# MLP down passes whose PSUM banks start from the sums so far, with more units by seven products

## The chip, the core and the metric

The kernel runs on one core of a Trainium2 chip. The metric is the device time of one execution in microseconds, the median of several. The profile is of one execution; TensorE is PE in it (its weight loads PEld), VectorE is DVE, ScalarE ACT, GpSimd POOL, and the queue of SyncE SP.

## What is computed

One layer of a trunk: a gated linear attention mixer, then a squared-ReLU MLP, each with an RMSNorm ahead and a residual behind, then a final RMSNorm. 256 tokens, 2048 channels, all float32. The change touches the MLP and the end only:

```python
def _sq_relu_mlp(h, w_up, w_down):      # w_up (2048, 8192), w_down (8192, 2048)
    a = jax.nn.relu(h @ w_up)
    return (a * a) @ w_down
...
    h = h + _sq_relu_mlp(_rmsnorm(h, mlp_norm[i]), mlp_w_up[i], mlp_w_down[i])
return _rmsnorm(h, final_norm)
```

## The kernel before

**Float32 from three products.** Each weight tile is loaded from HBM into a `raw` tile (six of them in turn). ACT writes its rounded part `hi`, DVE the rest `lo = raw - hi` (function `parts`, L117 and L118, for the down weights; `weights`, L137 and L141, for the up weights). A product is three matmuls: activation hi by weight hi, hi by lo, lo by hi. `hi` and `lo` each have five slots in turn (`slots`), so a new pair can be written when TensorE has done with the pair five before it. The activations are the stationary operand in the down passes; every matmul there has 256 columns.

**Rounds.** The hidden width of 8192 is cut into eight rounds m of 1024. `up` makes a round's hidden activations in 16 steps of 24 matmuls (two halves q of eight steps, each half with two PSUM banks). At the end of a half, `forms` takes each bank: a ReLU with the norm's factor on DVE (L700, tile `su`), the square on ACT (L704), and, where sums are needed, three subtractions on DVE (L708), then hi and lo of the result (L715, L716, tile `act`). Four such forms belong to a round.

**Down.** `down` walks through passes (m, g): round m, group g of 512 output columns. There are four groups in rounds 0 to 6, walked forward in odd rounds and backward in even ones (`order_of`), so that the last group of a round is the first of the next and the two passes share their banks; round 7 does only groups 0 and 1 in this way. A pass has four units kp, each one tile of 256 x 512 of `w_down`. One up step stands between two units, for as long as there are up steps: there are 128, and 18 are done ahead of the first unit, so the last ten of the 120 units have none.

**Two ways of a unit.** A plain unit multiplies a 2 x 2 arrangement of blocks with eight products, 24 matmuls. A unit by sums uses seven products of sums of blocks (the scheme of Strassen and Winograd), 21 matmuls: three products with the weights as loaded (9 matmuls, from 768 of the tile's 1024 columns), then four products with sums of weight blocks (12 matmuls). The sums are three additions on DVE (L770) into one of two `work` tiles, which then goes through hi and lo again (L117 and L118, the rows with `hi<-work` and `lo<-work`) into a slot of the ring. Which units go by sums is said by

```python
def by_sums(m, g, kp):
    if m == ROUNDS - 1:
        return (g, kp) in ((1, 0), (1, 2))
    return kp < (2 if g == 1 or m == ROUNDS - 2 else 3)
```

that is 11 of 16 units in rounds 0 to 5, eight in round 6, two of the eight in round 7: 76 in all.

**Banks.** A pass, or a pair of passes that share, adds up in four PSUM banks: `b16`, `b32`, `b57`, `bx4`. The first matmul in each overwrites. When the pass is over, its sums must be added to what earlier rounds left: `b32` and `bx4` to the two token halves of the residual `h` (`take`, L722), `b16` and `b57` to the group's `sums` (L802; the first time a plain copy on ACT, L800). These are additions on DVE out of PSUM, 23 passes' ends with four each; they are kept in `late` and put out two at a time by `settle` behind the next units. When a group is through, `combine` (L819, L823) adds its `sums` into `h`. PSUM has eight banks: four for the pass, two for the up step, and two that pass between them through the list `free`.

**The end.** The last two groups of round 7 are done in natural order (`last_step`) in five banks; each is added to `h` by `take` (L883), squared on ACT with a row sum (`finish`, L846) and multiplied by the final norm's gain on DVE (L848). From the row sums come `sf` (L886), its power -1/2 on POOL (`rsqrt`, L321), the scaling and the stores.

Engines execute their instructions in the order in which the build lays them down; an instruction that waits holds up those behind it on its engine. The build orders them itself within what `issue_after` prescribes.

Of the kernel before, what the change touches and what calls it, by code (L numbers as in the profile page):

```python
# [32 lines left out]
P = 128  # L33
T = 256
# [34 lines left out]
def tile_gla_mlp(ctx, tc, x, xt, cols, w_vg, w_in, w_gate, w_out, w_up, w_down, final_norm, out):  # L69
# [38 lines left out]
    last_load, last_hi, last_lo, last_sum = [None], [None], [None], [None]  # L108
# [4 lines left out]
    def parts(raw, n, to, pieces=None):  # L113

        hi, lo = to
        for s in (slice(*p) for p in pieces or [(0, n)]):
            last_hi[0] = nc.scalar.copy(hi[:, s], raw[:, s])  # L117
            last_lo[0] = nc.vector.tensor_tensor(lo[:, s], raw[:, s], hi[:, s].bitcast(F32), op=ALU.subtract)  # L118
        return hi, lo
# [4 lines left out]
    def weights(src, n, pieces=None, room=None, gap=None):  # L124
# [5 lines left out]
        for s in (slice(*p) for p in loads):  # L130
            dst = raw[:, s]
            if len(src.shape) == 3:
# [4 lines left out]
                last_hi[0] = nc.scalar.copy(to[0], dst)  # L137
# [530 lines left out]
    free = deque([*acc_free, *aux_free])  # L668

    def up():  # L670
        ended = []
        for m in range(ROUNDS):
            for q in range(MR // GT):
# [22 lines left out]
    def forms(m, kp, bank, act):  # L696
        ways = {by_sums(m, g, kp) for g in range(GROUPS)}
        f = work[:, 2].rearrange("p (f s) -> p f s", f=8)
# [4 lines left out]
        )  # L703
        nc.scalar.activation(  # L704
# [16 lines left out]
    def take(bank, t, lo, n):  # L721
        nc.vector.tensor_tensor(h[:, t, lo : lo + n], bank, h[:, t, lo : lo + n], op=ALU.add)  # L722

    left, right = slice(0, T), slice(T, 2 * T)
    used, begun = set(), set()
    n_sums = [0]

    def down(passes):

        late = []  # L730

        def settle(n=2):

            with tc.issue_after(last_lo[0].ins):
                for f in late[:n]:
                    f()
            del late[:n]

        for n, (m, g) in enumerate(passes):
            if not n or passes[n - 1][1] != g:  # L740
                taken = [free.popleft() for _ in range(2)]
                b16, b32 = (psum_bank(i) for i in taken)
                b57 = None
            ends = n + 1 == len(passes) or passes[n + 1][1] != g
            for kp in range(KP):
# [3 lines left out]
                def product(bank, o, a, w, c):  # L749
# [10 lines left out]
                w = parts(raw, 2 * GT, slots(), [(T * by_parts, 2 * GT)])  # L760
                if by_parts:
                    block = lambda i: slice(i * T, (i + 1) * T)
                    product(b16, left, at(A11), w, block(1))
                    product(b32, right, at(A12), w, block(3))
                    product(b32, left, at(S4), w, block(2))
# [10 lines left out]
                else:  # L776
                    for i in range(2):
                        for bank, f in ((b32, (A11, A12)), (bx4, (A21, A22))):
                            product(bank, slice(0, GT), at(f[i]), w, slice(i * GT, (i + 1) * GT))
                yield  # L780
                settle()
                if by_parts:
                    if b57 is None:
                        taken += [free.popleft() for _ in range(2)]
                        b57, bx4 = (psum_bank(i) for i in taken[2:])
# [3 lines left out]
                    product(b57, left, at(S1), wu, block(0))  # L789
                    product(b57, right, at(S3), wu, block(1))  # L790
                    product(b16, right, at(S2), wu, block(2))
                    product(bx4, right, at(A22), wu, block(3))
            if ends:

                e = sums[g]

                def keep(dst, b, first=g not in begun):
                    b = b.rearrange("p (f s) -> p f s", f=2)
                    if first:
                        nc.scalar.copy(dst, b)  # L800
                    else:
                        nc.vector.tensor_tensor(dst, b, dst, op=ALU.add)  # L802

                begun.add(g)
                fs = (
                    lambda keep=keep, b=b16, e=e: keep(e[:, 1:3], b),
                    lambda b=b32, g=g: take(b, 0, g * GT, GT),
                    lambda keep=keep, b=b57, e=e: keep(e[:, 0::3], b),
                    lambda b=bx4, g=g: take(b, 1, g * GT, GT),
                )  # L810
                late.extend(lambda f=f, i=i: (f(), free.append(i)) for f, i in zip(fs, taken))
                if m == ROUNDS - 1 or m == ROUNDS - 2 and g > 1:
                    late.append(lambda g=g: side.extend(combine(g)))
        settle(len(late))
# [15 lines left out]

    passes = [(m, g) for m in range(ROUNDS) for g in order_of(m) if m < ROUNDS - 1 or g < 2]
# [11 lines left out]

    def finish(t, lo, n):
        sq = tmp.tile([P, 512], F32, tag="t512", name="sqf", bufs=3)
        nc.scalar.activation(sq[:, :n], h[:, t, lo : lo + n], AF.Square, accum_out=fs[:, t, n_fs[t] : n_fs[t] + 1])  # L846
        n_fs[t] += 1
        nc.vector.tensor_tensor(hf[:, t, lo : lo + n], h[:, t, lo : lo + n], fb[:, lo : lo + n], op=ALU.mult)  # L848
# [86 lines left out]
```

## Time and profile before

| | |
|---|---|
| median of 3 runs | 1065.09 us (1065.07 to 1065.47) |
| profiled execution | 1064.77 us, of which 1062.8 us span |
| TensorE busy in the span | 1053.7 us |
| VectorE busy | 842.3 us |
| ScalarE busy | 590.2 us |
| HBM read | 206.92 MB, 197 GB/s |

A row of the groups has the line, the engine, the operation, output and inputs by the program's names, the shapes and the count; then busy time in us, the mean of one instruction in ns, and the idle time of the engine just before such instructions with what ended most of it. A row of the waits has who waited for whom, the total in us, how often, and the longest. A row of busy time by stretch has the stretch, its length, then the busy time of PE, PEld, DVE, ACT and POOL with the number of instructions in brackets, the granted clock, the DMA share and GB/s. A row of the timeline has start, length, engine and instruction. The busy time counts overlapping instructions of an engine once; the mean of a group is an instruction's own length. A matmul is pipelined: its own row shows 276 ns, while the next one starts after 113 ns.

### The profile page before, as it was taken

How to read it: one execution, taken by the hardware profiler on the slowest of the kernel's cores; microseconds unless marked ns; L12 is line 12 of the kernel's file. 1: busy time of each engine (PE TensorE's matmuls, PEld its weight loads, DVE VectorE, ACT ScalarE, POOL GpSimd, SP SyncE). 2: the span in 40 equal slices, each digit the busy share in tenths (PEclk: the TensorE clock that was granted, in tenths of full speed). 3: DMA queues.
4: the chain of work that ended last, by engine and by line, in shares of the span. 5: the costliest groups of instructions: out<-in, count | busy, mean ns of one | idle time of the engine just before them, and what ended most of it. 6: DMA issues, size and time to landing. Idle time of an engine off the chain costs nothing.

```text
span 1062.8 us, 22112 instructions
## 1 busy us (share of the span) xinstructions
PE 1053.7 (99%) x9202; PEld 1053.0 (99%) x9202; DVE 842.3 (79%) x1144; ACT 590.2 (56%) x723; POOL 13.2 (1%) x39
## 2 busy tenths in 40 slices
PE   9999999999999999999999999999999999999996
PEld 9999999999999999999999999999999999999996
DVE  5778644656555566898999999999999989979987
ACT  6785444545445454665655655655655556545454
POOL 0000000000000000000000000000000000000000
PEclk9999999999999999999999999999999999999999
DMA  9957765556656666666666666676667665666662
GB/s 337 325 164 218 198 189 155 160 156 178 196 180 185 184 179 187 174 194 200 213 214 194 201 202 198 198 229 191 193 198 223 194 203 186 213 198 198 211 220 86
DMA packets 94788, 210.45 MB, mean 198 GB/s; under 512 B 6704, under 2 KB 7600, under 8 KB 94560
## 3 DMA queue, kind: packets, MB, share of 16 engines
q1 hardware_dynamic: 93728, 206.99, 62.7%
q10 hardware_dynamic: 960, 2.05, 0.5%
q8 instruction: 72, 1.18, 0.5%
q14 instruction: 28, 0.23, 0.1%
HBM read 206.92 MB, written 2.10 MB: 197 GB/s over the span
## 4 chain that ended last, share of the span: by engine, by line
PE 97%; DMA 2%; issue 0%; SPq 0%; DVE 0%; ACT 0%; POOL 0%; POOLq 0%; DVEq 0%; ACTq 0%
PE acc L152 53%; PE up L189 33%; PE acc L189 6%; PE aux L189 2%; DMA raw<-in_w_vg 1%; PE aux L152 1%; PE aux L558 1%; DMA zz<-in_xt 1%; PE aux L486 1%; SPq L144 0%; DVE lo L118 0%; ACT hi L117 0%; POOL rf L321 0%; PE acc L387 0%; SPq L278 0%
## 5 line engine op out<-in xcount | busy, mean ns | idle before, releaser
L118 DVE TENSOR_TENSOR lo<-raw,hi 128x768 fp32r<-128x768 f32 (+3 forms) x226 | 251.5, 1115 | 124.4 <-ACT hi L117 123.5
L117 ACT CAST hi<-raw 128x768 fp32r<-128x768 f32 (+3 forms) x226 | 217.6, 965 | 202.5 <-PE acc L152 134.3
L152 PE MATMUL acc<-hi,act 128*128 128x256 f32 x1864 | 323.2, 276 | 0.0
L189 PE MATMUL up<-hl,hi 128*128 128x256 f32 x1024 | 282.9, 276 | 0.0
L189 PE MATMUL up<-hh,hi 128*128 128x256 f32 x1024 | 282.8, 277 | 0.0
L189 PE MATMUL up<-hh,lo 128*128 128x256 f32 x1024 | 282.5, 276 | 0.0
L152 PEld LDWEIGHTS acc<-hi,act 128*128 128x128 f32 x1864 | 274.7, 188 | 0.0
L137 ACT CAST hi<-raw 128x1024 fp32r<-128x1024 f32 x160 | 167.9, 1051 | 166.7 <-PE up L189 91.4
L141 DVE TENSOR_TENSOR lo<-raw,hi 128x1024 fp32r<-128x1024 f32 x160 | 195.2, 1222 | 46.2 <-ACT hi L137 39.6
L152 PE MATMUL acc<-lo,act 128*128 128x256 f32 x932 | 225.4, 276 | 0.0
L189 PEld LDWEIGHTS up<-hl,hi 128*128 128x128 f32 x1024 | 192.4, 188 | 0.0
L189 PEld LDWEIGHTS up<-hh,hi 128*128 128x128 f32 x1024 | 192.3, 188 | 0.0
L189 PEld LDWEIGHTS up<-hh,lo 128*128 128x128 f32 x1024 | 192.1, 188 | 0.0
L152 PEld LDWEIGHTS acc<-lo,act 128*128 128x128 f32 x932 | 160.6, 188 | 0.0
L117 ACT CAST hi<-work 128x1024 fp32r<-128x1024 f32 x76 | 80.1, 1054 | 47.6 <-DVE work L770 32.0
L152 PE MATMUL acc<-hi,xA 128*128 128x256 f32 (+1 forms) x736 | 105.3, 281 | 0.0
L118 DVE TENSOR_TENSOR lo<-work,hi 128x1024 fp32r<-128x1024 f32 x76 | 92.6, 1218 | 8.8 <-ACT hi L117 8.2
L152 PEld LDWEIGHTS acc<-hi,xA 128*128 128x128 f32 x736 | 94.4, 189 | 0.4 <-ACT hi L117 0.2
L770 DVE TENSOR_TENSOR work<-work,raw 128x256 f32<-128x256 f32 x152 | 64.2, 423 | 3.7
L152 PE MATMUL acc<-lo,xA 128*128 128x256 f32 (+1 forms) x368 | 58.6, 279 | 0.0
L770 DVE TENSOR_TENSOR work<-raw 128x512 f32<-128x512 f32 x76 | 51.9, 683 | 0.0
L152 PEld LDWEIGHTS acc<-lo,xA 128*128 128x128 f32 x368 | 49.8, 189 | 0.3 <-DVE lo L118 0.3
(151 smaller groups left out, 1098.0 us busy)
## 6 DMA issues: line engine op xcount, KB each, us to landing
raw<-in_w_up SPq DMA_DIRECT2D x128, 512.0 KB, 4.7
raw<-in_w_down SPq DMA_DIRECT2D x128, 512.0 KB, 4.1
raw<-in_w_in SPq DMA_DIRECT2D x80, 512.0 KB, 3.8
raw<-in_w_out SPq DMA_DIRECT2D x32, 512.0 KB, 3.7
raw<-in_w_vg SPq DMA_DIRECT2D x14, 520.0 KB, 8.4
h<-in_x SPq DMA_DIRECT2D x4, 512.0 KB, 9.1
zz<-in_xt SPq DMA_DIRECT2D x3, 384.0 KB, 8.4
fb<-in_final_norm ACTq DMA_DIRECT2D x1, 1024.0 KB, 4.9
```

Of the source, the lines that this page charges most:

```text
L117: last_hi[0] = nc.scalar.copy(hi[:, s], raw[:, s])
L118: last_lo[0] = nc.vector.tensor_tensor(lo[:, s], raw[:, s], hi[:, s].bitcast(F32), op=ALU.subtract)
L137: last_hi[0] = nc.scalar.copy(to[0], dst)
L141: last_lo[0] = nc.vector.tensor_tensor(to[1], dst, to[0].bitcast(F32), op=ALU.subtract)
L152: nc.tensor.matmul(o[:, m], x, w[:, m], start=first and c == 0, stop=last, skip_group_check=True)
L189: nc.tensor.matmul(o, u[:, i, s], m, start=kt == 0 and n == 0 and j % 2 == 0, stop=kt == KT - 1 and n == 2, skip_group_check=True,)
L486: nc.tensor.matmul(o, kab[:, k[0], c0 + c, k[1] : k[1] + P], q(qt[:, c0 + c]), start=c == 0, stop=c == 1)
L558: nc.tensor.transpose(b[:, o + t * P : o + (t + 1) * P], src[:, t, kt * P : (kt + 1) * P], ident)
L770: add = lambda o, x, y: nc.vector.tensor_tensor(o, x, y, op=ALU.add)
```

## The change

The sums so far are copied into a bank before the pass's first matmul (ACT), the matmuls add onto them, and at the end the bank is copied back whole (ACT). `take` and `keep` go. The first time that a group's `sums` are used, the bank still begins with an overwriting matmul. The copies are kept in one order by `last_end` and behind the last hi conversion laid down before them; later hi conversions are laid behind the copies (`copy_hi`). The banks of `h` for the next pass are taken and filled during the last unit of the pass before (`ahead`); those of `sums` during the new pass's unit kp 1, each right after two of the old banks are copied back.

Units by sums become 12 of 16 in round 0, 13 of 16 in rounds 1 to 6 (all four units of the group that a round begins with, kp 1 to 3 of the others), and units kp 1 and 3 of the two groups in round 7: 94 in all. The forms of an up half first normalize both banks, then do the rest. At the end, the last two groups' banks are filled with `h` beforehand; a fifth bank follows when one is free, and its products of the first two steps are done late. The last bank of each token half isn't copied back: the square and the gain read the bank.

```diff
-    last_load, last_hi, last_lo, last_sum = [None], [None], [None], [None]
+    last_load, last_hi, last_lo, last_sum, last_end = [None], [None], [None], [None], [None]
+
+    def copy_hi(to, raw):
+        with ExitStack() as order:
+            if last_end[0]:
+                order.enter_context(tc.issue_after(last_end[0]))
+            last_hi[0] = nc.scalar.copy(to, raw)
...
         if m == ROUNDS - 1:
-            return (g, kp) in ((1, 0), (1, 2))
-        return kp < (2 if g == 1 or m == ROUNDS - 2 else 3)
+            return g < 2 and kp % 2 == 1
+        return kp > 0 or m > 0 and g == order_of(m)[0]
...
+                    normal = [normalized(b) for b in acc]
                     for b in range(2):
-                        forms(m, 2 * q + b, acc[b], act[:, b])
+                        forms(m, 2 * q + b, normal[b], act[:, b])
...
-    def take(bank, t, lo, n):
-        nc.vector.tensor_tensor(h[:, t, lo : lo + n], bank, h[:, t, lo : lo + n], op=ALU.add)
...
+    def copy_end(to, src):
+        with tc.issue_after(last_hi[0].ins), ExitStack() as order:
+            if last_end[0]:
+                order.enter_context(tc.issue_after(last_end[0]))
+            last_end[0] = nc.scalar.copy(to, src).ins
...
+    def home(k, g):
+        if k in (P16, P57):
+            return sums[g][:, 1:3] if k == P16 else sums[g][:, 0::3]
+        return h[:, k // 2, g * GT : (g + 1) * GT].rearrange("p (f s) -> p f s", f=2)
...
+    def begin(k, g):
+        i = free.popleft()
+        bank = psum_bank(i)
+        if k in (B32, BX4) or g in begun:
+            copy_end(two(bank), home(k, g))
+            used.add(bank.name)
+        return i, bank
...
+            fresh = not n or passes[n - 1][1] != g
+            if fresh:
+                banks = ahead or {k: begin(k, g) for k in (B32, BX4)}
+                if m == ROUNDS - 1:
+                    flush()
...
+                if fresh and kp == 1:
+                    settle()
+                    banks[P16] = begin(P16, g)
+                if last:
+                    if n + 1 < len(passes):
+                        ahead = {k: begin(k, passes[n + 1][1]) for k in (B32, BX4)}
+                    else:
+                        acc[0][:] = [going_on(psum_bank(free.popleft()), h[:, 0, G + lo : G + hi]) for lo, hi in cuts[0]]
+                        acc[1][:] = [going_on(psum_bank(free.popleft())[:, : hi - lo], h[:, 1, G + lo : G + hi]) for lo, hi in cuts[1][:-1]]
...
                 yield
-                settle()
+                if fresh and kp == 1:
+                    settle()
+                    banks[P57] = begin(P57, g)
...
-                def keep(dst, b, first=g not in begun):
-                    b = b.rearrange("p (f s) -> p f s", f=2)
-                    if first:
-                        nc.scalar.copy(dst, b)
-                    else:
-                        nc.vector.tensor_tensor(dst, b, dst, op=ALU.add)
...
+                def end(k, i, bank, g=g):
+                    copy_end(home(k, g), two(bank))
+                    free.append(i)
...
-            take(acc[t][c][:, : hi - lo], t, G + lo, hi - lo)
-            finish(t, G + lo, hi - lo)
...
+            o = acc[t][c]
+            if hi < G:
+                copy_end(h[:, t, G + lo : G + hi], o)
+                finish(t, G + lo, hi - lo)
+                continue
...
+            square(t, o)
+            sf = st.tile([P, 1], F32, tag="sf", name="sf")
+            last = nc.vector.tensor_scalar(sf, fs[:, t, n_fs[t] - 1 : n_fs[t]], 1.0 / D, some, op0=ALU.mult, op1=ALU.add)
+
+            with tc.issue_after(last.ins):
+                times_gain(t, o, G + lo)
```

More of the change, by code (lines that the diff above doesn't have):

```diff
@@ L694, in up, with normalized @@
         ended.pop()()
-    def forms(m, kp, bank, act):
-        ways = {by_sums(m, g, kp) for g in range(GROUPS)}
-        f = work[:, 2].rearrange("p (f s) -> p f s", f=8)
+    def normalized(bank):
         s = tmp.tile([P, 2, T], F32, tag="t512", name="su", bufs=3)
@@ L703, in forms @@
         )
+        return s
+    def forms(m, kp, s, act):
+        ways = {by_sums(m, g, kp) for g in range(GROUPS)}
+        f = work[:, 2].rearrange("p (f s) -> p f s", f=8)
         nc.scalar.activation(
```

108 lines of the change are left out of this document (57 added, 51 removed).

## The prediction

> **What bounds the kernel now.** First the page: the span, the busy line, the chain that ended last.
>
> ```profile
> span 1062.8 us, 22112 instructions
> PE 1053.7 (99%) x9202; PEld 1053.0 (99%) x9202; DVE 842.3 (79%) x1144; ACT 590.2 (56%) x723; POOL 13.2 (1%) x39
> PE 97%; DMA 2%; issue 0%; SPq 0%; DVE 0%; ACT 0%; POOL 0%; POOLq 0%; DVEq 0%; ACTq 0%
> ```
>
> TensorE never waits, so the time is its number of matmuls, and every wait put into its stream is lost. Next the table of busy time by stretch: two rounds of the MLP, the piece after the last up step, and the end.
>
> ```profile
> core 0: us, PE busy (x) PEld busy (x) DVE busy (x) ACT busy (x) POOL busy (x), PEclk, DMA share, GB/s
> 673.19:756.57 83.38, 83.38 (x737) 83.38 (x736) 78.63 (x106) 47.91 (x52) 0.00 (x0) 1.00 0.64 203
> 839.95:923.33 83.38, 83.38 (x737) 83.38 (x736) 78.69 (x106) 47.92 (x52) 0.00 (x0) 1.00 0.64 202
> 988.00:1062.80 74.80, 66.81 (x590) 66.62 (x588) 62.59 (x99) 35.85 (x51) 1.48 (x2) 0.97 0.50 168
> 1002.50:1031.00 28.50, 28.50 (x254) 28.50 (x253) 24.43 (x32) 16.11 (x19) 0.00 (x0) 1.00 0.62 205
> ```
>
> A matmul takes 83.38 / 737 = 0.113 us. The vector engine is 94% busy in a round: only 4.7 us are free, so it is the second bound. Then the waits:
>
> ```profile
> ACT hi L117 <- PE acc L152: 136.9, 107, 2.0
> DVE lo L118 <- ACT hi L117: 131.7, 132, 1.9
> ACT hi L117 <- DVE work L770: 32.0, 29, 3.5
> ```
>
> ACT converts (hi) as soon as TensorE gives a slot back, DVE follows (lo): the ring of five slots is full, and that is the cover. Conversion k waits for the release of slot k-5; four slots lie between, in a stretch of sums 54 to 69 matmuls (9, 24, 12, then 9 or 24), 6.1 to 7.8 us; less hi 1.05 and lo 1.22 (below), lo is 3.8 to 5.5 us early.
>
> **What operations cost.** Groups by line, kept apart by form:
>
> ```profile
> L141 DVE TENSOR_TENSOR lo<-raw,hi 128x1024 fp32r<-128x1024 f32 x160 | 195.2, 1222 | 46.2 <-ACT hi L137 39.6 <-PE acc L152 4.8 <-PE aux L558 0.6
> L118 DVE TENSOR_TENSOR lo<-work,hi 128x1024 fp32r<-128x1024 f32 x76 | 92.6, 1218 | 8.8 <-ACT hi L117 8.2
> L118 DVE TENSOR_TENSOR lo<-raw,hi 128x768 fp32r<-128x768 f32 x76 | 72.5, 954 | 14.8 <-ACT hi L117 14.6
> L770 DVE TENSOR_TENSOR work<-work,raw 128x256 f32<-128x256 f32 x152 | 64.2, 423 | 3.7
> L770 DVE TENSOR_TENSOR work<-raw 128x512 f32<-128x512 f32 x76 | 51.9, 683 | 0.0
> L722 DVE TENSOR_TENSOR h<-acc,h 128x512 f32<-128x512 f32 x49 | 33.3, 682 | 0.5 <-PE acc L152 0.4
> L802 DVE TENSOR_TENSOR sums<-acc,sums 128x512 f32<-128x512 f32 x38 | 26.0, 683 | 0.0
> L700 DVE SCALAR_TENSOR_TENSOR su<-up,work 128x512 f32<-128x512 f32 x32 | 21.4, 685 | 0.0
> L716 DVE TENSOR_TENSOR act<-work,act 128x896 fp32r<-128x896 f32 x14 | 15.1, 1082 | 0.0
> L708 DVE TENSOR_TENSOR work<-work 128x128 f32<-128x128 f32 x44 | 12.5, 285 | 0.3
> L716 DVE TENSOR_TENSOR act<-work,act 128x1024 fp32r<-128x1024 f32 x8 | 9.7, 1217 | 0.0
> L708 DVE TENSOR_TENSOR work<-work 128x256 f32<-128x256 f32 x22 | 9.2, 417 | 0.0
> L716 DVE TENSOR_TENSOR act<-work,act 128x512 fp32r<-128x512 f32 x10 | 6.8, 683 | 0.0
> L117 ACT CAST hi<-work 128x1024 fp32r<-128x1024 f32 x76 | 80.1, 1054 | 47.6 <-DVE work L770 32.0
> L549 ACT ACTIVATE sr<-acc,r 128x512 f32<-128x512 f32 x8 | 5.2, 690 | 0.8 <-PE acc L152 0.7
> L715 ACT CAST act<-work 128x512 fp32r<-128x512 f32 x10 | 6.2, 622 | 0.3
> L800 ACT COPY sums<-acc 128x512 f32<-128x512 f32 x8 | 4.3, 584 | 0.0
> ```
>
> And the timeline of one unit, for the hand-overs:
>
> ```profile
> 604.03 0.96 DVE L118 TENSOR_TENSOR lo<-raw,hi 128x768 fp32r<-128x768 f32 x1 [0.82 <-ACT hi L117]
> 604.90 0.68 DVE L770 TENSOR_TENSOR work<-raw 128x512 f32<-128x512 f32 x1
> 605.62 0.89 DVE L770 TENSOR_TENSOR work<-work,raw 128x256 f32<-128x256 f32 x2
> 606.60 1.05 ACT L117 CAST hi<-work 128x1024 fp32r<-128x1024 f32 x1 [0.91 <-DVE work L770]
> 607.68 1.23 DVE L118 TENSOR_TENSOR lo<-work,hi 128x1024 fp32r<-128x1024 f32 x1
> ```
>
> Neighbours on DVE overlap by 0.09 us (0.96 long, the next starts after 0.87), adds that depend on each other don't; adds to hi takes 0.09, hi to lo 0.03. A unit by sums costs DVE 0.95 + 0.68 + 2 x 0.42 + 1.22 = 3.70, a plain one 1.22.
>
> **The change, part by part.**
>
> 1. Matmuls. Units by sums go from 76 to 94 (12 + 6 x 13 + 4). Each has 21 matmuls instead of 24: 18 x 3 = 54 fewer, x 0.113 = -6.1 us, exact as long as TensorE doesn't wait.
>
> 2. DVE over the whole MLP: the adds of L722 and L802 go, -60 us; 18 units x (3.70 - 1.22) = +45; seven more forms with sums (three subtractions 0.99, 896 for 512 wide 0.40) = +10. Net -6 us; in a round 94% becomes 93%. Little relief, and none is needed, by these totals.
>
> 3. ACT gets 89 fills of banks and 87 copies back, 0.58 each as in the L800 row: in a round 24 x 0.58 less overlaps, 48 + 14 = 62 of 82.6 us, hidden by total. A fill (SBUF to PSUM) isn't in the trace; it lies between 0.50 (the 0.584 less the 0.08 that overlap hides) and 0.69 (L549); nearest are L800 and L715, and I take 0.584. [...]
>
> 4. Where ACT stands still. At a pass end the copy back waits for TensorE's last product in that bank, and all later hi conversions queue behind it, so DVE starves. Two settles hold ACT for 8 x (0.58 - 0.10) = 3.9 us, out of the 3.8 to 5.5 us of cover: 0 to 1.6 remain; nearer to the upper, since ACT has idle time between, I take 1.2. Then the merged run follows: the last three units of a round and the first four of the next are now all by sums. Each, with its up step, is 3.70 + 1.22 - 0.26 = 4.66 on DVE against 45 x 0.113 = 5.09; seven are 32.6, plus two forms of 0.69 + 0.99 + 1.08 - 0.3 = 2.45 each, together 37.5 against 35.6. Over by 1.9; less the cover, 0.7. Before, plain units stood in that run (3 us gained at each). There are six such runs, and the first comes while banks of `sums` need no fill yet: five, +3.5 us (bounds 0 with full cover, 9.5 with none).
>
> 5. After the last up step. Up has 128 steps, 18 run ahead, so units 110 to 119 have none beside them. Before, two of these ten were by sums (the 1002.50 row: DVE 24.4 of 28.5). Now six are: TensorE 6 x 21 + 4 x 24 = 222 matmuls, 25.1 us; DVE 6 x 3.70 + 4 x 1.22 + two forms 4.3, less overlaps 3 = 28.4, plus the waits: the next sums can't be added until the hi of this work tile, queued on ACT ahead of the next weights, is done. That loop is hi 1.05, lo work 1.22, lo plain 1.22, lo 0.95, adds 0.68 + 0.85, hand-overs 0.2, less overlaps 0.25 = 5.9 us per pair of units against 45 x 0.113 = 5.1. Four pairs 3.2; units 110 to 111 without a plain one between, 4.7 against 2.4: 2.3; the forms 3.8 less the gaps of the loop that they fill, 2.0; copies in between, 0.5. Sum 8.0; the run before has left 0.5 of cover: +7.5 (bounds 2.5 with the full cover, 9.8 with none and all forms on the loop).
>
> 6. The end.
>
> ```profile
> 1054.85 0.42 DVE L722 TENSOR_TENSOR h<-acc,h 128x256 f32<-128x256 f32 x1
> 1055.31 0.42 ACT L846 ACTIVATE sqf<-h 128x256 f32<-128x256 f32 x1 [1.16 <-DVE h L722]
> 1055.63 0.19 ACT L846 ACTIVATION_READ_ACCUMULATOR sqf<-h 128x1 f32 x1
> 1055.85 0.21 DVE L886 TENSOR_SCALAR sf<-fs,some 128x1 f32<-128x1 f32 x1
> 1056.15 0.55 POOL L321 TENSOR_TENSOR rf<-sf,mhalf 128x1 f32<-128x1 f32 x1 [3.55 <-DVE sf L886]
> ```
>
> The last add (start to start 0.46) goes; the square reads the bank; the multiplication by the gain moves behind sf, where the 0.55 us on POOL covers its 0.42. -0.5 us (bounds -0.5, 0). DMAs are neither more nor moved.
>
> Sum against the profiled execution's 1064.8 (span 1062.8 and 2.0 around it): -6.1 + 3.5 + 7.5 - 0.5 = +4.4, 1069.2; the median is 0.3 above that execution: 1069.5. Ends: -6.1 + 0 + 2.5 - 0.5 gives 1061; -6.1 + 9.5 + 9.8 gives 1078.
>
> **Rivals.**
>
> A, TensorE stays the bound: DVE falls by 6 us in all and ACT has a quarter free, so all lateness stays inside the ring; 1065.1 - 6.6 = 1058.5. It decides if some 8 us of cover stand at unit 110; against it, the ring gives 5.5 at most, and DVE's 28.4 exceeds TensorE's 25.1 even without waits.
>
> B, a near draw: the runs of part 4 stay covered (the copies fall into ACT's idle time), part 5 costs 5.5 to 7.5: 1064 to 1066. For it: the 107 waits of ACT on TensorE are slack that copies may use.
>
> C, fills and copies near 0.69: 0.1 x 24 a round more where no cover is left, up to 2.4 in each of six rounds, some 8 in all: 1077. For it: a fill is a form that the trace lacks; against it, L800 is the same copy in one direction.
>
> **How the numbers follow.** About 2 us (0.2%) is what can be told from no change: faster is below 1063.0, slower above 1067.2. Forecast (1067 to 1073) 0.56, A 0.14, B 0.16, C (1073 to 1080) 0.14. So faster 0.14, same 0.16, slower 0.70. The range for 8 in 10 cuts A's core and C's far end: 1062 to 1075.
>
> **What would show it.** TensorE idle near 11 us, of which more than half in the ten units after the last up step, put down to hi or to work; before that, short waits on hi once a round near the forms. In those ten units DVE waiting on ACT about 1.1 us per unit by sums, and ACT on work. ACT near 705 us busy, fills at 0.55 to 0.62. TensorE's busy time lower by 6.1. Wrong if it shows no idle at all (A), idle only at the end (B), or waits at each pass end on a filled bank (C).

## The result, and the profile after

| | before | after |
|---|---|---|
| median | 1065.08 us (1064.36 to 1065.47, 4 runs) | 1078.73 us (1077.62 to 1079.92, 4 runs) |
| profiled execution, and its span | 1064.77, 1062.8 us | 1079.18, 1077.1 us |
| matmuls | 9202 | 9148 |

The changed kernel is slower: ratio 1.0129, 95% interval 1.0112 to 1.0147, that is +13.65 us. The forecast was +4.4 us, its range ended at 1075: direction right, size wrong. First the page of the changed kernel, the same three lines as before:

```profile
span 1077.1 us, 22212 instructions
PE 1061.8 (99%) x9148; PEld 1058.2 (98%) x9148; DVE 834.9 (78%) x1148; ACT 677.0 (63%) x917; POOL 12.8 (1%) x39
PE 87%; DVE 7%; issue 2%; DMA 2%; ACT 1%; SPq 0%; ACTq 0%; POOLq 0%; POOL 0%; DVEq 0%
```

TensorE has 54 matmuls fewer and is busy for 8.1 us more. Busy time is therefore not the number of matmuls times a constant any more, and the share of 99% hides it. The busy time by stretch shows where; it has to be read as length by count:

```profile
core 0: us, PE busy (x) PEld busy (x) DVE busy (x) ACT busy (x) POOL busy (x), PEclk, DMA share, GB/s
525.00:599.00 74.00, 74.00 (x655) 74.00 (x655) 66.33 (x91) 52.92 (x71) 0.00 (x0) 1.00 0.61 200
611.00:692.00 81.00, 81.00 (x689) 81.00 (x690) 72.10 (x99) 57.68 (x76) 0.00 (x0) 1.00 0.61 200
695.00:778.00 83.00, 83.00 (x708) 83.00 (x707) 73.55 (x101) 59.04 (x77) 0.00 (x0) 1.00 0.61 195
864.00:938.00 74.00, 73.84 (x651) 73.64 (x650) 67.02 (x91) 53.44 (x71) 0.00 (x0) 1.00 0.62 200
950.00:1014.00 64.00, 64.00 (x546) 64.00 (x544) 57.57 (x81) 44.99 (x63) 0.00 (x0) 1.00 0.61 200
1014.00:1045.00 31.00, 26.55 (x206) 24.68 (x205) 25.07 (x36) 20.95 (x30) 0.00 (x0) 1.00 0.50 157
1046.00:1067.00 21.00, 21.00 (x181) 21.00 (x180) 18.15 (x31) 13.07 (x25) 0.55 (x1) 1.00 0.27 98
```

From 525 to 599 us a matmul takes 74.00 / 655 = 113.0 ns, as before the change. From 611 to 692 it takes 117.6, from 695 to 778 117.2, from 950 to 1014 117.2, and from 1046 to the end 116.0, with TensorE never idle in these stretches and the granted clock (the number after POOL) at 1.00. A stretch counts the matmuls that its two ends cut, so these quotients come out a little short, by 0.3% to 1.5% here; start to start the two spacings are 113.3 and 117.8 ns. Only the row from 1014 to 1045 has much idleness: 206 matmuls, 23.3 us of work at 113 ns, in 31.0.

The starts of single matmuls in the trace give the bill. From 440 us to the last matmul, before and after:

- fewer matmuls: -5.9 us;
- gaps in the stream: +8.5 us, of which 7.1 behind 1014 us and 1.4 in seven waits of 0.03 to 0.44 us at the starts of three rounds (600 to 611, 855 to 866, 938 to 949 us);
- 2580 matmuls start 115 to 123 ns after the one before them, where 89 did before: +11.1 us;
- from the last matmul to the end of the span: 8.3 us before, 8.8 after, +0.5.

Together +14.2 of the +14.3 by which the span grew. The third item is the one that the prediction doesn't have. The stretches of long spacing begin at the waits (at 610.84 and 949.33 us behind waits of 0.44 and 0.42, at 600.11 behind one of 0.03), not at a pass end or a filled bank. (A wait is counted here wherever a start comes more than 0.02 us late.)

The costs of ACT's new work, from the groups by form:

```profile
L744 ACT COPY h<-acc 128x512 f32<-128x512 f32 x48 | 28.8, 600 | 1.6 <-PE acc L158 1.6
L744 ACT COPY sums<-acc 128x512 f32<-128x512 f32 x46 | 27.3, 594 | 47.6 <-PE acc L158 47.6
L744 ACT COPY acc<-h 128x512 f32<-128x512 f32 x49 | 27.0, 583 | 0.0
L744 ACT COPY acc<-sums 128x512 f32<-128x512 f32 x38 | 23.4, 616 | 0.0
```

Fills take 583 to 616 ns, copies back 594 to 600. ACT stands 47.6 us at the first copy back of pass ends, until TensorE is through; that alone costs nothing, since the kernel with 82 units below stands there 49.1 us and has no gap. What changed for the hi conversions shows in the waits:

```profile
ACT hi L114 <- PE acc L158: 109.2, 77, 2.0
ACT hi L114 <- DVE work L821: 95.6, 55, 3.2
```

Before, ACT mostly waited for a free slot (136.9 us for the down weights alone, to which L117 belongs) and rarely for DVE's sums (32.0). Now it waits 95.6 us for the sums. Between 441 and 1005 us alone, the waits of hi conversions for a slot fell from some 200 us to 15, and those for sums rose from 25 to 88: DVE is late more often, and the ring isn't full. One such place is the wait at 610 us, here in the timeline of ACT:

```profile
609.74 1.05 ACT L114 CAST hi<-work 128x1024 fp32r<-128x1024 f32 x1 [2.91 <-DVE work L821]
...
611.43 0.59 ACT L744 COPY acc<-h 128x512 f32<-128x512 f32 x1
```

ACT had nothing to do for 2.91 us ahead of that hi: DVE, busy without a gap from 594 us on, was late with the sums. The next copy stands behind it, so no copy held it up. After the last up step the same view shows the loop of the prediction's part 5:

```profile
1017.16 1.04 ACT L114 CAST hi<-work 128x1024 fp32r<-128x1024 f32 x1 [0.22 <-DVE work L821]
...
1024.09 1.04 ACT L114 CAST hi<-work 128x1024 fp32r<-128x1024 f32 x1 [3.25 <-DVE work L821]
...
1030.02 1.05 ACT L114 CAST hi<-work 128x1024 fp32r<-128x1024 f32 x1 [2.20 <-DVE work L821]
...
1033.67 0.59 ACT L744 COPY sums<-acc 128x512 f32<-128x512 f32 x1 [0.92 <-PE acc L158]
...
1036.63 1.08 ACT L114 CAST hi<-work 128x1024 fp32r<-128x1024 f32 x1
```

From hi to hi 6.93 us (a form lies in it), 5.93, then 6.61 (six copies lie in it), against 5.1 that TensorE needs for a pair of units. And the end:

```profile
1067.55 0.56 ACT L744 COPY h<-acc 128x512 f32<-128x512 f32 x1
...
1068.14 0.63 ACT L887 ACTIVATE sqf<-h 128x512 f32<-128x512 f32 x1
...
1068.77 0.35 ACT L744 COPY h<-acc 128x256 f32<-128x256 f32 x1
...
1069.57 0.36 ACT L887 ACTIVATE sqf<-acc 128x256 f32<-128x256 f32 x1
...
1070.44 0.55 POOL L327 TENSOR_TENSOR rf<-sf,mhalf 128x1 f32<-128x1 f32 x1 [3.99 <-DVE sf L946]
```

The last square no longer waits for an add, but for two copies back and two squares that stand ahead of it on ACT.

### The profile page after: what moved, and what is told of

It is laid out like the page before. It is cut to its first block, busy times and chain, and to the rows that moved or that the text cites. A ratio compares the mean times of both kernels' runs of the same rounds, so it can differ in the third digit from the quotient of the medians.

```text
span 1077.1 us, 22212 instructions
## 1 busy us (share of the span) xinstructions
PE 1061.8 (99%) x9148; PEld 1058.2 (98%) x9148; DVE 834.9 (78%) x1148; ACT 677.0 (63%) x917; POOL 12.8 (1%) x39
## 4 chain that ended last, share of the span: by engine, by line
PE 87%; DVE 7%; issue 2%; DMA 2%; ACT 1%; SPq 0%; ACTq 0%; POOLq 0%; POOL 0%; DVEq 0%
PE acc L158 47%; PE up L195 30%; PE acc L195 6%; DVE lo L124 3%; PE aux L195 2%; DVE work L821 2%; ACT hi L114 1%; DVE lo L147 1%; DMA raw<-in_w_vg 1%; PE aux L158 1%; PE aux L564 1%; DMA zz<-in_xt 1%; PE aux L492 1%; DVE act L729 0%; DVE work L721 0%
## 5 line engine op out<-in xcount | busy, mean ns | idle before, releaser
L114 ACT CAST hi<-raw 128x1024 fp32r<-128x1024 f32 (+3 forms) x386 | 373.6, 991 | 173.8 <-PE acc L158 108.5
L158 PE MATMUL acc<-hi,act 128*128 128x256 f32 x1828 | 336.7, 278 | 4.9 <-ACT hi L114 4.8
L124 DVE TENSOR_TENSOR lo<-raw,hi 128x1024 fp32r<-128x1024 f32 (+3 forms) x226 | 246.3, 1092 | 105.7 <-ACT hi L114 105.1
L195 PE MATMUL up<-hh,lo 128*128 128x256 f32 x1024 | 271.4, 278 | 0.0
L195 PEld LDWEIGHTS up<-hh,lo 128*128 128x128 f32 x1024 | 186.7, 188 | 0.0
L114 ACT CAST hi<-work 128x1024 fp32r<-128x1024 f32 x94 | 99.5, 1058 | 107.7 <-DVE work L821 95.6
L124 DVE TENSOR_TENSOR lo<-work,hi 128x1024 fp32r<-128x1024 f32 x94 | 114.8, 1221 | 24.8 <-ACT hi L114 23.4
L821 DVE TENSOR_TENSOR work<-work,raw 128x256 f32<-128x256 f32 x188 | 79.5, 423 | 4.5
L821 DVE TENSOR_TENSOR work<-raw 128x512 f32<-128x512 f32 x94 | 64.3, 684 | 0.0
L744 ACT COPY sums<-acc 128x512 f32<-128x512 f32 x46 | 27.3, 594 | 47.6 <-PE acc L158 47.6
```

The lines of the kernel that those rows point to most:

```text
L114: last_hi[0] = nc.scalar.copy(to, raw)
L158: nc.tensor.matmul(o[:, m], x, w[:, m], start=first and c == 0, stop=last, skip_group_check=True)
L195: nc.tensor.matmul(o, u[:, i, s], m, start=kt == 0 and n == 0 and j % 2 == 0, stop=kt == KT - 1 and n == 2, skip_group_check=True,)
L744: last_end[0] = nc.scalar.copy(to, src).ins
L821: add = lambda o, x, y: nc.vector.tensor_tensor(o, x, y, op=ALU.add)
```

## The experiments

What had to be settled: whether 118 ns is a consequence of waits, of the new order of matmuls, or of banks that ACT fills; and how the waits divide between ACT's copies and the 18 more units by sums. One thing of the code matters here that the prediction took no notice of. In one step of each round (`even` in `up`) the weights are laid out with `gap`, which puts 16 elements between the two halves of the tile (`between` in `weights`, 1088 - 48 - 1024). In the trace of before, the last twelve matmuls of this step (by the order of the code those on the half that lies further on) are the only ones in a round that start 120 ns apart; here is the busy time of before by stretch, over one such dozen and behind it:

```profile
606.90:608.22 1.32, 1.32 (x13) 1.32 (x12) 1.29 (x2) 0.74 (x1) 0.00 (x0) 1.00 0.33 37
608.40:690.00 81.60, 81.60 (x723) 81.60 (x722) 76.39 (x105) 46.73 (x51) 0.00 (x0) 1.00 0.65 206
```

In between (606.93 to 608.25 us) the starts are 119 to 121 ns apart, before and behind them 113. In the changed kernel the stretches of 118 ns end at this step, at 607, 779, 862 and 945 us, though the one at 693 us changed nothing.

The trace of before has the long spacing too, but ahead of the MLP, where I hadn't divided anything. One place is behind a row of matmuls of 128 columns; there the start behind 249.67 us comes 201 ns later, and then:

```profile
249.67 0.71 PE L152 MATMUL acc<-hi,xA 128*128 128x256 f32 x4
250.22 0.63 PE L152 MATMUL acc<-lo,xA 128*128 128x256 f32 x4
250.69 0.51 PE L152 MATMUL acc<-hi,xA 128*128 128x256 f32 x3
```

Four matmuls take the 0.47 us from 250.22 to 250.69, 117.5 ns each. From 249.9 to 255.2 us 46 starts are 117.8 ns apart on average, from 266 to 294 us 248 starts 113.3, with the granted clock at 1.00 in both.

**Old units, new copies (e1_old_units).** 76 units by sums in the changed kernel:

```diff
         if m == ROUNDS - 1:
-            return g < 2 and kp % 2 == 1
-        return kp > 0 or m > 0 and g == order_of(m)[0]
+            return (g, kp) in ((1, 1), (1, 3))
+        return kp > (1 if g == 1 or m == ROUNDS - 2 else 0)
```

> The changed kernel with as many units by sums as the kernel before (76, in the places that its new bank scheme allows: the last two or three units of a pass instead of the first). Theory: ACT's fills and copies back cost nothing by themselves, all the loss comes from the 18 added units by sums; so 1064 to 1066 us, no gap of TensorE over 0.1 us between 440 and 1055 us, and 113 ns from matmul to matmul throughout. Rival (fills and copies themselves hold ACT and through it TensorE): 1068 to 1074 us, with gaps at pass ends.

Measured 1070.63 us, ratio 1.0066 (1.0042 to 1.0090), with all loss behind 1010 us; that is the rival's time, though the rounds show nothing of it. Up to there no gap, and 83.00 us for 734 matmuls from 690 to 773 us as before the change: in the rounds the copies cost nothing. Behind 1010 us they do, as the timeline of ACT in this kernel shows:

```profile
1018.26 1.05 ACT L728 CAST act<-work 128x1024 fp32r<-128x1024 f32 x1 [0.38 <-DVE work L721]
1025.19 0.59 ACT L744 COPY h<-acc 128x512 f32<-128x512 f32 x1 [5.88 <-PE acc L158]
...
1027.14 0.61 ACT L744 COPY acc<-sums 128x512 f32<-128x512 f32 x1
1027.66 1.06 ACT L114 CAST hi<-work 128x1024 fp32r<-128x1024 f32 x1
```

The sums for the next unit were ready at 1021.6 us, but their hi stands behind five copies that wait 5.88 us for TensorE's last product of the pass; it runs at 1027.66, and TensorE waits for it until 1028.8. That is the standing still of the prediction's part 4, at a place for which it wasn't priced. The test isn't pure: the new bank scheme puts four units by sums behind the last up step, not two. The profiled execution, 1075.8 us, had one more wait, 2.9 us up to 1049, behind the late load of the final gain, and slow matmuls behind it (last section); the other three took 1070.1 to 1071.1.

**94 units, old adds (e2_adds_94).** In the kernel before:

```diff
         if m == ROUNDS - 1:
-            return (g, kp) in ((1, 0), (1, 2))
-        return kp < (2 if g == 1 or m == ROUNDS - 2 else 3)
+            return g < 2 and kp % 2 == 0
+        return kp < 3 or m > 0 and g == order_of(m)[-1]
```

> The kernel before (sums of the banks added by the vector engine) with 94 units by sums in place of 76, some of them at other places than in the changed kernel. Theory: DVE then needs 569.5 us (its busy time from 441 to 1063 us before) + 45 for 18 more units + 10 for seven more forms with sums = 624 us of the 616 that TensorE needs there, so TensorE waits in every round, the spacing of matmuls is 118 ns in most of them: 1080 to 1100 us, worse than the changed kernel. That is, ACT's copies are what makes 94 units bearable at all. Rival (the copies by ACT are the loss, the units are not): 1059 to 1068 us.

Measured 1086.36 us, 1.0206 (1.0190 to 1.0221), inside the theory's range, but TensorE doesn't wait in every round: it waits at 610.2 and 864.8 us, for 0.2 to 0.3 us, without any of ACT's new copies, and nearly all its other loss, some 12 us of gaps, lies behind 990 us. The first of the two waits is followed by some 1430 matmuls at 118 ns, the second by some 700. The stretches ahead of the first and behind it, in this kernel's busy time by stretch:

```profile
524.00:607.00 83.00, 83.00 (x734) 83.00 (x733) 79.37 (x111) 49.16 (x55) 0.00 (x0) 1.00 0.63 200
607.00:690.00 83.00, 83.00 (x706) 82.89 (x705) 80.63 (x115) 47.31 (x52) 0.00 (x0) 1.00 0.60 195
```

So the waits at round starts belong to the run of seven units by sums, and the long spacing belongs to neither filled banks nor copies.

**A wait alone, and a short matmul alone (e4_three_waits, e5_no_waits).** In the kernel before, in rounds 2, 4 and 6; the first has the inner memset, the second doesn't. Only zeros are added.

```diff
                     product(bx4, right, at(A22), wu, block(3))
+                hold[0] = None
+                if (m, g, kp) in [(2, 0, 1), (4, 0, 1), (6, 0, 1)]:
+                    for _ in range(2):
+                        nc.gpsimd.memset(z.bitcast(F32), 0.0)
+                        with after():
+                            hold[0] = nc.tensor.matmul(bx4[:, :32], at(A22)[0], z, start=False, stop=False, skip_group_check=True).ins
```

(`after` lays all matmuls that follow behind `hold[0]`, so that the order is otherwise that of before; in both traces the 9202 other matmuls stand in the order of before.)

> The kernel before with three waits of TensorE put in, in the third, fifth and seventh round: two matmuls of 32 columns of zeros into a bank that is being added up, with a memset of the zeros by GpSimd between them, for which the second one waits. No other engine takes part. Theory: each costs its wait (0.4 to 1.2 us) and then 4.4 ns for each matmul up to the next step with the shifted weights or further, 200 to 700 matmuls, 1 to 3 us: in all 4 to 12 us more than the kernel before, and stretches of 117 to 118 ns behind each wait. Rival (a wait costs itself alone): 1 to 4 us more and 113 ns throughout.

> The same as e4_three_waits without the memsets between: the six matmuls of 32 columns alone, no wait. Theory: it is the wait that changes the spacing, so this is within 1 us of the kernel before, 113 ns throughout. Rival (a short matmul in the stream is enough to shift the spacing): stretches of 117 to 118 ns as in e4_three_waits, 3 to 9 us more.

Measured 1070.16 us (1.0050; 1.0035 to 1.0065) with waits, and 1068.89 us (1.0039; 1.0025 to 1.0053) without. The busy time of the first by stretch:

```profile
609.00:671.00 62.00, 62.00 (x550) 62.00 (x549) 58.28 (x79) 33.80 (x37) 0.00 (x0) 1.00 0.63 200
673.00:691.00 18.00, 18.00 (x155) 18.00 (x154) 16.03 (x24) 10.03 (x13) 0.00 (x0) 1.00 0.59 188
693.00:774.00 81.00, 81.00 (x717) 81.00 (x717) 76.15 (x104) 46.56 (x50) 0.00 (x0) 1.00 0.64 205
1010.00:1058.00 48.00, 48.00 (x410) 48.00 (x409) 40.52 (x63) 22.66 (x34) 0.93 (x1) 1.00 0.40 135
```

112.7 ns up to the disturbance at 672 us, 116.1 behind it, 113.0 again from the shifted step at 692 us on. The third disturbance, at 1009 us, has no such step behind it: 117.1 ns to the end. In all 3 x 0.4 us of waits, and some 750 matmuls by about 4.4 ns: 3.3 us. The second kernel has the same stretches without a wait for another engine, here the one behind its first disturbance:

```profile
673.00:691.00 18.00, 18.00 (x155) 18.00 (x155) 16.37 (x24) 10.58 (x13) 0.00 (x0) 1.00 0.62 203
```

My theory held for the size and fell in one point: it needn't be a wait for another engine. Two matmuls of 32 columns break the even pace as well (behind them one start comes 208 ns after the last, 0.1 us late), and that too sets TensorE to the longer spacing. Since the matmuls and their order are those of before, neither order nor banks nor copies can be the reason here.

**The shifted step three steps later (e3_reset_later).** The changed kernel with `(6,) if q == 0` in place of `(3,) if q == 0`.

> The changed kernel, and one thing more: the step of each up pass whose weights lie 16 elements apart (the twelve matmuls of 120 ns once a round) comes three steps later, behind the place where TensorE waits in the rounds of 610, 865 and 949 us. Theory: these twelve matmuls bring the spacing of matmuls back from 117.7 to 113.3 ns, whatever broke it; the long stretches of 117.7 (2540 matmuls) shrink to some 190 in each of three rounds and 430 at the end, so 1500 x 4.4 ns = 6.6 us go: 1071 to 1074 us, with the same gaps. Rival (the spacing follows from the order of the matmuls or from the filled banks, and the step has nothing to do with it): 1078 to 1080 us.

Measured 1077.76 us (1075.09 to 1080.70), 1.0123 (1.0101 to 1.0144); the theory's 1071 to 1074 wasn't reached, and the time can't be told from the changed kernel's. The profiled execution is the fastest of the four. The step did move the end of the long spacing, to 624, 791 and 876 us; the first of them in this kernel's busy time by stretch:

```profile
600.00:624.00 24.00, 23.93 (x203) 23.72 (x202) 21.35 (x29) 16.10 (x22) 0.00 (x0) 1.00 0.71 230
625.00:682.00 57.00, 57.00 (x506) 57.00 (x504) 52.46 (x74) 39.93 (x54) 0.00 (x0) 1.00 0.60 193
```

That is 118.2 ns, then 112.6. But at 959 us it ended nothing; and at full pace TensorE met the wait of 0.35 us in each of five rounds instead of three: by this count the long spacing is also slack in which DVE catches up. Of 11.1 us, 3.7 went in this execution; the end was disturbed anew, with 1.6 us lost to matmuls 213 ns apart (last section).

**Thirteen a round, none behind the last up step (e8_thirteen_no_tail).** The changed kernel with

```diff
         if m == ROUNDS - 1:
-            return g < 2 and kp % 2 == 1
+            return False
+        if m == ROUNDS - 2 and g == 0:
+            return kp == 1
         return kp > 0 or m > 0 and g == order_of(m)[0]
```

> The changed kernel with 13 of 16 units by sums in the rounds as it is, but none of the ten units behind the last up step by sums (88 in all). Theory: the 7.5 us of waits behind 1014 us go, 18 matmuls come back (2.0 us), and the stretches of 118 ns from 610 and 949 us stay: 1072 to 1075 us. Rival (the waits in the last stretch come from the copies, not from the sums): they stay, 1079 to 1082 us.

Measured 1074.48 us, 1.0096 (1.0081 to 1.0111), as the theory has it. Gaps sum to 1.2 us in this execution, the longer spacing of 3029 matmuls to 13.7 us: what follows the waits costs eleven times their length. The last row of its busy time by stretch:

```profile
977.00:1063.00 86.00, 86.00 (x730) 86.00 (x731) 63.01 (x86) 55.58 (x85) 0.55 (x1) 1.00 0.52 172
```

117.8 ns, behind one wait of 0.25 us at 976.9.

**The same with more shifted steps (e10_more_resets).** `(3, 5, 7) if q == 0 or m == ROUNDS - 1` in place of `(3,) if q == 0`.

> e8_thirteen_no_tail (1074.5 us, 3029 matmuls at 118 ns) with more steps of shifted weights: three instead of one in the first up pass of a round, and three in each up pass of the last round. Nothing else is changed, and each added step costs twelve matmuls 7 ns, 0.084 us, 15 of them 1.3 us. Theory: the same short waits, but the spacing comes back to 113 ns within two to four steps of each, some 1000 matmuls at 118 ns are left: 1074.5 - 2000 x 0.0044 + 1.3 = 1067 us (1064 to 1070). Rival (the spacing is a matter of 13 units a round or of filled banks): 1075 to 1077 us. Back at full pace TensorE may also meet waits in rounds that had none: then 2 us more than the theory's figure, with new gaps at the round starts.

Measured 1069.07 us, 1.0038 (1.0025 to 1.0051). There are now waits at five round starts, 2.7 us in all, as the last sentence of the expectation has it, and yet 5.4 us are saved, since 950 matmuls are left at the long spacing. The same row for this kernel, behind its shifted steps:

```profile
1008.00:1057.00 49.00, 49.00 (x434) 49.00 (x434) 31.08 (x44) 30.63 (x51) 0.55 (x1) 1.00 0.44 149
```

112.9 ns with the same units, the same filled banks and, in both traces, the same 9166 matmuls in the same order. This settles that the spacing isn't theirs.

**Tail by sums with the old adds (e9_tail_sums_adds).** In the kernel before:

```diff
         if m == ROUNDS - 1:
-            return (g, kp) in ((1, 0), (1, 2))
+            return (g, kp) in ((0, 1), (0, 3), (1, 0), (1, 2))
+        if m == ROUNDS - 2 and g == 0:
+            return kp != 1
```

> The kernel before, all sums of the banks by the vector engine, with six of the ten units behind the last up step by sums in place of two (79 in all, one more of them just before it). Theory: the loop of work, hi, lo and the next sums, 5.9 us for a pair of units against TensorE's 5.1, gives the waits without any copy of ACT: 1064.8 - 1.0 for nine matmuls + 5 to 7.5 for waits + some 1.5 for 118 ns in the last 45 us: 1070 to 1073 us. Rival (the copies make the waits of the last stretch): 1063.5 to 1066 us.

Measured 1077.27 us, 1.0117 (1.0100 to 1.0134): the rival fell, and the theory's figure is exceeded by 4. Up to 1010 us there is no gap; behind it, in its busy time by stretch:

```profile
1010.00:1040.00 30.00, 25.50 (x176) 23.84 (x175) 26.04 (x35) 15.63 (x18) 0.00 (x0) 0.89 0.46 145
```

176 matmuls, 19.9 us of work, in 30.0, at a granted clock of 0.89. Units by sums without up steps between them stop TensorE with or without ACT's copies.

**Twelve a round, none at the end (e6_twelve_no_tail).** The changed kernel with `return False` for the last round and `return kp == 1 if m == ROUNDS - 2 and g == 0 else kp > 0` for the others.

> The changed kernel with 82 units by sums: the first unit of a round is plain again (12 of 16), and none of the ten units behind the last up step is by sums. Theory: plain units stand again between the runs, so no wait before 1005 us, 113 ns throughout, no loop of work, hi and lo in the last ten units: 1064.8 - 18 x 0.113 - 0.5 = 1062.3 us (1061 to 1064). Rival (ACT standing at the copies back of the last passes still starves TensorE, as in e1_old_units from 1010 us on): 1065 to 1069 us, with gaps on hi of 0.5 us and more there.

Measured 1062.83 us (10 runs), 0.9985 (0.9976 to 0.9995): 0.15% below the kernel before and clear of its interval, as the theory has it. No gap, 113 ns throughout, as its busy time by stretch shows:

```profile
774.00:855.00 81.00, 81.00 (x717) 81.00 (x717) 70.91 (x96) 57.57 (x76) 0.00 (x0) 1.00 0.64 205
940.00:988.00 48.00, 48.00 (x426) 48.00 (x425) 42.76 (x60) 34.51 (x48) 0.00 (x0) 1.00 0.62 194
990.00:1051.00 61.00, 61.00 (x541) 61.00 (x540) 41.70 (x56) 39.07 (x63) 0.55 (x1) 1.00 0.49 164
```

**Three tries beyond it (e11_thirteen_odd, e12_two_tail, e13_odd_and_tail).** Thirteen in the odd rounds only (`kp > 0 or m % 2 == 1 and g == order_of(m)[0]`); twelve with two units at the end (`return g < 2 and kp == 1` for the last round); and both.

> e6_twelve_no_tail with the first unit of the second, fourth and sixth round by sums too (85 units), so every other round has the run of seven. Theory (each run of seven uses up cover that a round with a plain unit gives back): no wait, 113 ns throughout, 1062.8 - 3 x 0.34 = 1061.8 us. Rival (a run of seven at full pace ends in a wait every time, as from 854 us on after the slower rounds): waits of 0.3 to 0.5 us at two or three round starts, each followed by 700 matmuls or more at 118 ns: 1067 to 1073 us.

> e6_twelve_no_tail with two of the ten units behind the last up step by sums, four units apart (84 units). Theory: plain units (DVE 1.22 of 2.7 us) on both sides take up each of them, no wait: 1062.8 - 0.7 = 1062.1 us. Rival (each unit by sums there, with its work tile waiting on ACT behind the copies of a pass end, stops TensorE for 0.5 to 1 us, and 118 ns follows to the end): 1064 to 1067 us.

> e11_thirteen_odd and e12_two_tail together (87 units). Theory: both free of waits, 1062.8 - 1.0 - 0.7 = 1061.1 us. Rival: the sum of what the two show of losses, 1066 us and more.

Measured 1069.83 us (1.0055; 1.0034 to 1.0075), 1065.06 us (1.0000; 0.9992 to 1.0009) and 1071.43 us (1.0064; 1.0052 to 1.0076). The theory fell in all three. The first try waits at 683 and 694 us, 0.5 us together, at the second of its three runs of seven, and 1550 matmuls at the longer spacing follow: one run of seven at full pace can be enough, though the first of them, at some 527 us, passed without a wait. The second try is the plainest case of all. Its only disturbance is 0.2 us at 989 us, and of the two stretches on its sides, in its busy time by stretch,

```profile
940.00:988.00 48.00, 48.00 (x426) 48.00 (x426) 42.90 (x61) 33.78 (x47) 0.00 (x0) 1.00 0.60 193
990.00:1053.00 63.00, 63.00 (x537) 63.00 (x536) 47.39 (x66) 42.01 (x66) 0.55 (x1) 1.00 0.49 165
```

the first has 112.7 ns and the second 117.3. The view of waits lists nothing for TensorE between 441 and 1060 us. The rival's mechanism fell as well: this wait stands 13 us ahead of the last up step (1002 us), not at one of the two added units. Because these two need sums of activations, the last round's forms grow, as the timeline of DVE shows:

```profile
968.29 0.42 DVE L721 TENSOR_TENSOR work<-work 128x256 f32<-128x256 f32 x1
...
977.66 1.22 DVE L729 TENSOR_TENSOR act<-work,act 128x1024 fp32r<-128x1024 f32 x1 [0.47 <-ACT act L728]
```

With two more subtractions at 971.23 and 974.37 us, DVE starts the lo of the unit in question at 989.40 us, against 988.36 in the kernel with 82 units, which has no such forms there.

**Shifted steps behind that wait (e15_tail_resets).** The kernel of the second try with `(5, 7) if (m, q) == (ROUNDS - 1, 1)` put ahead in `even`.

> e12_two_tail (1065.1 us: one wait of 0.2 us at 989 us, then 548 matmuls at 118 ns) with steps of shifted weights at the sixth and eighth step of the last up pass, where it has none. Theory: the wait stays, the spacing comes back to 113 ns by 996 or 1006 us, 400 to 480 matmuls x 4.4 ns go and 24 x 7 ns come: 1063.0 to 1063.5 us. Rival (the spacing is due to the two units by sums or to the filled banks of the last passes): 1065 to 1065.5 us.

Measured 1064.38 us, 0.9998 (0.9989 to 1.0007). The wait at 990 us is there, and the second of the two steps brings the spacing back: 178 matmuls in 20.00 us from 1004 to 1024 us, 112.4 ns. Then a second wait, 0.2 us at 1025 us, sets it to 117 again up to the end. The medians differ by 0.7 us where 1.6 to 2.1 were expected, and half of that is the kernel before, which was 0.3 us faster beside this run: by time no gain is shown. What happened in each stretch fits the theory, the figure doesn't.

**Twelve a round with the old adds (e14_twelve_adds).** In the kernel before, `return (g, kp) == (1, 0)` for the last round and `kp < (1 if m == ROUNDS - 2 and g == 0 else 3)` for the others, 83 units.

> The kernel before (adds by the vector engine) with 12 of 16 units by sums in a round and one of the ten units behind the last up step: 83 units, one more than e6_twelve_no_tail, which has 1062.8 us with ACT's copies. Theory (the vector engine's relief of some 7 us a round is what lets a round have 12): DVE then needs 77 + 2.5 + forms 1.2 = 81 of the 82.5 us of a round, and with runs of three and the adds in a row TensorE waits at some round starts, 118 ns follows: 1066 to 1073 us. Rival (12 a round need no relief, the copies bring nothing): 1062 to 1063 us, 113 ns throughout.

Measured 1065.60 us (1063.01 to 1066.56), 1.0006 (0.9997 to 1.0015). My theory fell: DVE is busy 79.87 of 83.00 us in its rounds, and TensorE doesn't wait there. The one wait of the profiled execution, 0.7 us, comes at 984 us, with 118 ns to the end. ACT stood waiting for sums there:

```profile
983.19 1.05 ACT L117 CAST hi<-work 128x1024 fp32r<-128x1024 f32 x1 [4.06 <-DVE work L770]
```

So twelve a round need no copies. The wait stands at the end of round 6, where DVE has both the grown forms of the last round (L708 at 966.40 us) and the old adds (L802 and L722 at 969.55, 970.15, 977.69 and 978.29 us) to do; the version at 1062.83 has neither. Which of the two makes its quiet end is not shown: no run has the old adds with no unit by sums in the last round.

## Why the prediction missed

The step that failed is in parts 4 and 5, and in the clause of part 1, "exact as long as TensorE doesn't wait": each wait was priced at its own length, and each matmul at 0.113 us whatever came before it. The runs showed that a break of the pace sets the matmuls behind it to about 117.7 ns until a step with shifted weights, or longer. In the changed kernel that is 11.1 us, more than the waits. Without it the bill would be +3.1 us, near the forecast +4.4, and that partly by luck: part 4 was 2.1 us too dear and part 6 1.0 too cheap. The trace of before held the signs: stretches of 118 ns ahead of the MLP, and twelve matmuls of 120 ns in each round, for which I had no reason.

- **1, matmuls:** the count is right; -5.9 us.
- **2, DVE:** -6 forecast over the MLP, 842.3 to 834.9 us measured over the span.
- **3, ACT's prices:** right, 0.58 to 0.62 us. ACT is busy 677.0 us instead of 705, since more of its work overlaps (61 us, before 25): copies in a row start 0.48 to 0.52 us apart (1033.67, 1034.15, 1034.63, 1035.15). Hidden in the rounds, as forecast (e1_old_units: 113 ns up to 1010 us). Copies on ACT in place of adds on DVE don't show as a loss: with 94 units, partly at other places, adds took 1086.36 us and copies 1078.73.
- **4, the merged runs:** the place is right and the reason half right. DVE's overload in the run of seven makes the waits, not ACT's standing still, since they are there with the old adds too. The size is wrong: 1.4 us, in three of the five runs, not 3.5 in all, and then the spacing.
- **5, the last ten units:** right. Waits of 7.5 us forecast, 7.1 measured; a loop of 5.9 us forecast, 5.93 measured.
- **6, the end:** wrong in sign, +0.5 instead of -0.5: two copies back and two squares were not counted on ACT's queue.

Rival A fell, there was no spare cover at the end; so did B. C has nearly the right time (1077) for the wrong reason: fills are not dearer, and the rounds hide them. The upper end of the sum, 1078, is near the result by chance too: it has waits of 19.3 us, of which 8.5 came. Of the signs listed, TensorE's idle time came out as 8.5 us in gaps (11 forecast), most of it in the last ten units and put down to hi, and short waits at round starts. "TensorE's busy time lower by 6.1" failed openly, at +8.1: that one line of the page refutes the sum.

Left open: when the shifted step ends the long spacing. Over all traces it met the long spacing 40 times and ended it 31 times; at 693 us in the changed kernel and at 959 us in the one with the later step it didn't. Open too are why the wait at 865 us in the changed kernel wasn't followed by the long spacing, while the same wait in the kernel without sums at the end was; why in the kernel with the later step a wait at 694 us brought the short spacing back; and what in TensorE or its operands' addresses keeps the two spacings apart.

## What to carry to other kernels

Before pricing a wait on the bounding engine, divide stretch lengths by instruction counts over the whole trace of before, not only where the change is: if the same instruction comes at two paces, a wait costs its length and all that follows at the worse pace, here from three times its length (the three waits put in) to fourteen (thirteen in the odd rounds). A change that takes 0.3 us from each of many units can pay only while the stream stays unbroken, so stop short of the first wait: 82 units gave 1062.83 us, 94 gave 1078.73. And an average load of 90% says nothing for the stretch in which the helpers are overloaded; there, count the longest run of heavy units.

## What the runs showed of the hardware

At a granted clock of 1.00 and with no gap, the same matmul (128 x 128 by 256 columns) came every 113.3 or every 117.8 ns on average, start to start, hundreds in a row. A wait of 0.03 us (changed kernel, 600.11 us) or two matmuls of 32 columns (e5_no_waits: 116.1 ns by count behind them) could switch from the one to the other; matmuls with weights laid out 16 elements further apart came every 120 ns and switched back in 31 of 40 cases.

Longer waits cost in yet another way: behind waits of 1.9 to 2.9 us, 10 to 29 matmuls came every 213 ns in four kernels, 1.0 to 2.9 us more (e1_old_units, e2_adds_94, e3_reset_later and e9_tail_sums_adds: the mean granted clock of their profiled executions is 0.994 to 0.996, before it is 0.998). The granted clock was 0.50 behind the wait of 2.9 us in the kernel with old units and new copies (the 0.89 in the row of the tail with the old adds is the mean of 30 us with such a stretch in them):

```profile
1049.70:1055.20 5.50, 5.50 (x28) 5.50 (x27) 5.50 (x9) 0.72 (x2) 0.00 (x0) 0.50 0.01 1
```

The waits had others close by: in the tail with the old adds there were eight between 1005 and 1045 us, 6.1 us together, the longest 2.7. What sets the slower clock off is not shown: in the changed kernel's own profile, with waits of up to 1.9 us and a granted clock of 1.00 from 1014 to 1045 us, it didn't happen.
